# An encoder block on one core: the transpose of a feed-forward unit's result moved one weight chunk later

## The chip, the cores and the metric

The kernel runs on one core of a Trainium2 chip. The metric is the device time of one execution in microseconds (us). TensorE (PE) multiplies, VectorE (DVE) and ScalarE (ACT) do elementwise work, GpSimd (POOL) a few small things, and SyncE (SP) issues most loads. Each engine works through its own instructions in the order in which the program issues them.

## What is computed

One layer of an encoder over 256 positions of width 2048, in float32: a gated feed-forward with half weight, a mixer, a second gated feed-forward with half weight, and a final norm.

```python
def swiglu(h, w_gate, w_up, w_down):
    return (jax.nn.silu(h @ w_gate) * (h @ w_up)) @ w_down

x = x + 0.5 * swiglu(rmsnorm(x, ffn1_norm), ffn1_w_gate, ffn1_w_up, ffn1_w_down)
...   # mixer: input projection, pooling branch, convolution branch, gates, output projection
x = x + 0.5 * swiglu(rmsnorm(x, ffn2_norm), ffn2_w_gate, ffn2_w_up, ffn2_w_down)
out = rmsnorm(x, final_norm)
```

The feed-forward is 5632 wide; its three weights are 2048x5632, 2048x5632 and 5632x2048. The change touches the two feed-forward stages alone.

## The kernel before

**Numbers in two words.** Every operand of a product is split into a high word (a rounded copy, made by a cast on ScalarE) and a low word (the rest, made by a subtraction on VectorE): `hi_lo`, lines 154 and 156. A product is three matmuls: high by high (data high, weight high), then data high by weight low, then data low by weight high. In the profile weights are `raw` as loaded, then `wh` and `wl`.

**Units and chunks.** The weights stream through in chunks of two tiles of 128x1024. A `Unit` is a run of chunks that adds up to 256x1024 results in PSUM: a gate unit has 8 chunks (512 gate columns and the 512 up columns beside them), a half of a down projection 8 chunks (6 in the last one). A feed-forward stage consists of gate units 0 to 10; behind gate units 4 and 8, and at the end, two halves of a down projection take the hidden units made so far. In all gate units but unit 0, and in the down projections but the last, chunks 0 and 2 are calculated as a 2x2 block product with seven multiplications (`SEVEN = (0, 2)`): `split_seven` makes four sums of weight blocks on VectorE (line 194, tile `sum`) and splits three tiles (the first weight tile, the sums as `exth`/`extl`, the second weight tile). Such a chunk has 21 matmuls (line 278), any other 24 (line 257). In unit 1 of each stage the seven products come in another order: those that need the sums first.

**The order of work.** It is written out by hand. `run` goes through the chunks; for chunk i it issues, in this order, the loads of chunk i+2 on SP's queue, the splitting of chunk i+1, the functions that were left for i with `at(i, ...)`, and the matmuls of chunk i. So each engine has the splitting of the next chunk ahead of the side work of the present one. There are 5 buffers for loaded tiles and 4 each for `wh` and `wl`, two chunks' worth.

**A hidden unit's way.** When a gate unit u is done, at its chunk 7, `gate_done_seven` adds the partial results on VectorE (line 431), applies Silu on ScalarE (line 432) and multiplies (line 436): two tiles `h` of 128x512, one for each half of the positions. The down projection needs them transposed. `turn` (line 386) has ScalarE separate the 16-bit halves of `h` (line 391, tile `halves`) and issue a DMA transpose (line 393, tile `turned`), once for each of the two tiles. `put` (line 397) has ScalarE join the transposed halves (line 403, tile `hy`) and splits the result in two words into `ht` (`hi_lo`). For some units (those with u mod 4 equal to 0 or 1) `put` leaves `e_forms` (line 303) for the chunk after: four subtractions on VectorE (line 308, tile `e`) and their splitting into `hEh` and `hEl`, for the seven-product chunks of the down projection.

In time: `turn` of unit u stands in chunk 0 of the unit that follows. `gate_early` runs in chunk 3 of a gate unit, takes what was turned last, and leaves its `put` for chunk 4; `e_forms` comes in chunk 5. Unit 10 has no gate unit behind it; its `put` is left by `rest_of_hidden`, in chunk 3 of the last down projection.

Of the kernel before, what the change touches and what calls it, by code (L numbers as in the profile page):

```python
# [18 lines left out]
FF = 5632  # L19
# [7 lines left out]
C = 512  # L27
# [55 lines left out]
def encoder_kernel(ctx: ExitStack, tc: tile.TileContext, x, xT, vecs, rows, pool_m,  # L83
# [30 lines left out]
    def at(i, fn):  # L114

        side.setdefault(i, []).append(fn)
# [36 lines left out]
    def hi_lo(src, h, l=None):  # L153
        nc.scalar.copy(out=h, in_=src)  # L154
        if l is not None:
            nc.vector.tensor_tensor(out=l, in0=src, in1=h.bitcast(F32), op=ALU.subtract)  # L156
        return h, l
# [145 lines left out]
    def e_forms(dst, even, odd):  # L303

        e = stg.tile([P, 4, P], F32, tag="sg", name=f"e{Pos.now}")
        a11, a21, a12, a22 = even[:, :P], even[:, P:], odd[:, :P], odd[:, P:]
        for n, (a, b) in enumerate(((a11, a21), (a21, a22), (a11, e[:, 1, :]), (a12, e[:, 2, :]))):
            nc.vector.tensor_tensor(out=e[:, n, :], in0=a, in1=b, op=ALU.subtract)
        hi_lo(e, *dst)
# [67 lines left out]
    def ffn_units(w_g, w_d, xt, xE, rs, residual_done, tail=None):  # L377
# [8 lines left out]
        def turn(u, hs):  # L386

            turned = []
            for t in range(NT):
                halves = ffn["pool"].tile([P, 2, C], U16, tag=f"halves{t}", name=f"halves{Pos.now}_{t}")  # L390
                nc.scalar.copy(out=halves, in_=hs[t].bitcast(U16).rearrange("p (f w) -> p w f", w=2))  # L391
                z = ffn["pool"].tile([P, 8, P], U16, tag=f"turned{t}", name=f"turned{Pos.now}_{t}")
                nc.scalar.dma_start_transpose(out=z, in_=halves.rearrange("p w f -> p (w f)"))  # L393
                turned.append(z)
            waiting.append((u, turned))

        def put(u, turned):

            y = ffn["pool"].tile([P, 4, T], F32, tag="y", name=f"hy{Pos.now}")
            whole = y.bitcast(U16).rearrange("p j (t w) -> p w j t", w=2)  # L400
            for t in range(NT):
                for w in range(2):
                    nc.scalar.copy(out=whole[:, w, :, t * P:(t + 1) * P], in_=turned[t][:, 4 * w:4 * w + 4, :])  # L403
            hi_lo(y, *ffn["ht"][u % GROUP])
            for c in SEVEN:
                if c // 2 == u % GROUP:
                    q = c % 2 * 2
                    at(Pos.now + 1, lambda c=c, q=q: e_forms(ffn["hE"][c], y[:, q, :], y[:, q + 1, :]))

        def hidden_tile(t):  # L410
            return stg.tile([P, C], F32, tag="h", name=f"h{Pos.now}_{t}")

        def gate_done(u):
            def done(acc):
                hs = []
                for t in range(NT):
                    sg = stg.tile([P, C], F32, tag="sg", name=f"sg{Pos.now}_{t}")
                    h = hidden_tile(t)
                    nc.scalar.activation(sg, acc[t][:, 0, :], AF.Silu, scale=rs[:, t:t + 1])
                    nc.vector.scalar_tensor_tensor(out=h, in0=acc[t][:, 1, :], scalar=rs[:, t:t + 1],  # L420
                                                   in1=sg, op0=ALU.mult, op1=ALU.mult)
                    hs.append(h)
                at(Pos.now + 1, lambda: turn(u, hs))
            return done

        def gate_done_seven(u):
            def done(acc):
                hs = []
                for t in range(NT):
                    z = ffn[f"t{t}"]  # L430
                    nc.vector.tensor_tensor(out=z, in0=acc[t], in1=z, op=ALU.add)  # L431
                    nc.scalar.activation(z[:, 0, :], z[:, 0, :], AF.Silu, scale=rs[:, t:t + 1])
                for t in range(NT):
                    z = ffn[f"t{t}"]
                    h = hidden_tile(t)
                    nc.vector.scalar_tensor_tensor(out=h, in0=z[:, 1, :], scalar=rs[:, t:t + 1],
                                                   in1=z[:, 0, :], op0=ALU.mult, op1=ALU.mult)
                    hs.append(h)
                at(Pos.now + 1, lambda: turn(u, hs))
            return done  # L440

        def shared_parts():

            z0, z1 = ffn["t0"], ffn["t1"]
            nc.scalar.copy(out=z0[:, 0, :], in_=ps[:, B_P1, :])
            for out, a, b, op in ((z1[:, 1, :], ps[:, B_P6, :], z0[:, 0, :], ALU.subtract),
                                  (z0[:, 1, :], ps[:, B_P5, :], z1[:, 1, :], ALU.add),
                                  (z1[:, 0, :], ps[:, B_P7, :], z1[:, 1, :], ALU.subtract),
                                  (z1[:, 1, :], z0[:, 1, :], ps[:, B_P7, :], ALU.subtract)):
                nc.vector.tensor_tensor(out=out, in0=a, in1=b, op=op)  # L450

        def gate_early():
            shared_parts()
            if waiting:
                u, turned = waiting.pop()
                at(Pos.now + 1, lambda: put(u, turned))

        def into_residual(t, half, part):
            xs = X[t][:, half * W2:(half + 1) * W2]
# [37 lines left out]
        for u in range(units):  # L497
            if u:
                add_unit(Unit(w_g[u], KD, lhs_of(xt), gate_done_seven(u), forms=forms_of(lhs_of(xt), xE),
                              early=gate_early, seven=SEVEN, start=(lambda: None) if u == 1 else None))  # L500
            else:
                first = Unit(w_g[u], KD, lhs_of(xt), gate_done(u))
                add_unit(first)
                at(len(stream), open_hidden)
            if u and u % GROUP == 0:
                add_down(u // GROUP - 1, 4 * GROUP, False)
# [519 lines left out]
```

## Time and profile before

| | |
|---|---|
| median of 3 runs | 1961.78 us (1959.55 to 1965.18) |
| profiled execution | 1962.23 us, span 1960.4 us |
| granted TensorE clock, mean | 0.997 |
| DMA transposes | 44, from issue to landing 7.5 / 10.0 / 12.4 us (min, median, max) |
| loads of feed-forward weights | 512 KB each, 4.4 us (gate and up) and 4.3 us (down) median to landing |

The span runs from the first to the last recorded instruction. In rows of instructions stand start, duration, engine, line, operation, what it writes and reads, the shapes, how many were merged, and in brackets how long the engine stood idle before it and what ended that. Rows of the chain of waits have start, duration and what; the chain is followed back from the last instruction. `ACTq` and `SPq` are the sequencers of ScalarE and SyncE, which issue DMAs. A matmul's row is longer than the step from one to the next, since they overlap.

### The profile page before, as it was taken

What the parts mean: (1) busy time and instruction counts of PE and PEld (TensorE: products, weight loads), DVE (VectorE), ACT (ScalarE), POOL (GpSimd) and SP (SyncE); (2) the same over time, 40 slices, a digit from 0 to 9 for tenths busy, and PEclk for the clock granted to TensorE, in tenths of its full rate; (3) what the DMA queues carried; (4) which work ended last, traced back from release to release, by engine and by line L of the source; (5) the groups of instructions that cost most, each with busy time, mean ns of one, the idle gap of its engine ahead of it and who ended that gap; (6) DMA issues with size and microseconds to landing.
All of it is one profiled execution on the core that took longest, in us unless ns stands there. A gap on an engine that the chain in (4) does not pass through costs nothing.

```text
span 1960.4 us, 23002 instructions
## 1 busy us (share of the span) xinstructions
PE 1924.6 (98%) x8504; PEld 1579.2 (81%) x8504; DVE 1517.1 (77%) x1740; ACT 1065.3 (54%) x1215; POOL 11.3 (1%) x22
## 2 busy tenths in 40 slices
PE   9999999999999999999999999999999999999998
PEld 7777788778787888888888888877778877778776
DVE  6788787888888655888898766688788788888865
ACT  6655645555555555454444545556654556654554
POOL 0000000000000000000000000000000000000000
PEclk9999999999999999999999999999999999999999
DMA  8777766777767756556666555567786577676774
GB/s 312 196 193 199 193 227 198 200 210 201 197 201 196 221 183 203 193 197 213 200 209 198 191 183 185 185 197 196 194 210 226 195 204 203 193 209 205 196 200 156
DMA packets 152608, 395.42 MB, mean 202 GB/s; under 512 B 58384, under 2 KB 58640, under 8 KB 152240
## 3 DMA queue, kind: packets, MB, share of 16 engines
q1 hardware_dynamic: 104688, 378.45, 58.6%
q10 hardware_dynamic: 46752, 11.68, 8.1%
q0 software_dynamic: 1056, 3.83, 0.6%
q8 instruction: 66, 1.08, 0.2%
q14 instruction: 46, 0.38, 0.1%
HBM read 380.28 MB, written 2.10 MB: 195 GB/s over the span
## 4 chain that ended last, share of the span: by engine, by line
PE 83%; ACT 6%; DVE 4%; DMA 3%; issue 2%; ACTq 2%; DVEq 0%; POOLq 0%; POOL 0%
PE ps L257 73%; PE ps L278 9%; ACT wh L154 2%; DMA raw<-in_w_g 2%; ACTq L393 2%; DVE extl L156 2%; ACT exth L154 2%; ACT halves L391 1%; DMA raw<-in_w_d 1%; DVE wl L156 1%; PE ps L344 1%; ACT hy L403 0%; PE ps L758 0%; DVE part L431 0%; DMA xrh<-in_xT 0%
## 5 line engine op out<-in xcount | busy, mean ns | idle before, releaser
L156 DVE TENSOR_TENSOR wl<-raw,wh 128x1024 fp32r<-128x1024 f32 (+1 forms) x706 | 842.4, 1219 | 294.1 <-ACT wh L154 293.1
L154 ACT CAST wh<-raw 128x1024 fp32r<-128x1024 f32 (+1 forms) x706 | 726.2, 1048 | 615.5 <-PE ps L257 314.2
L257 PE MATMUL ps<-wh,xt1h 128*128 128x512 f32 x544 | 168.5, 391 | 1.2 <-ACT wh L154 1.2
L257 PE MATMUL ps<-wl,xt1h 128*128 128x512 f32 x544 | 168.4, 390 | 0.2
L257 PE MATMUL ps<-wh,xt1l 128*128 128x512 f32 x544 | 168.4, 391 | 0.0
L257 PE MATMUL ps<-wh,xt3h 128*128 128x512 f32 x544 | 167.7, 389 | 0.0
L257 PE MATMUL ps<-wh,xt3l 128*128 128x512 f32 x544 | 167.5, 389 | 0.0
L257 PE MATMUL ps<-wl,xt3h 128*128 128x512 f32 x544 | 167.5, 389 | 0.0
L257 PE MATMUL ps<-wh,xt2h 128*128 128x512 f32 x448 | 138.4, 390 | 0.0
L257 PE MATMUL ps<-wh,xt2l 128*128 128x512 f32 x448 | 138.0, 389 | 0.0
L257 PE MATMUL ps<-wl,xt2h 128*128 128x512 f32 x448 | 138.0, 389 | 0.0
L257 PEld LDWEIGHTS ps<-wh,xt1h 128*128 128x128 f32 x544 | 102.6, 189 | 23.1 <-ACT wh L154 1.7
L257 PEld LDWEIGHTS ps<-wl,xt1h 128*128 128x128 f32 x544 | 102.3, 188 | 22.2 <-DVE wl L156 1.0
L257 PEld LDWEIGHTS ps<-wh,xt1l 128*128 128x128 f32 x544 | 102.3, 188 | 21.8 <-DVE xt1l L336 0.5
L257 PEld LDWEIGHTS ps<-wl,xt3h 128*128 128x128 f32 x544 | 102.1, 188 | 21.2
L257 PEld LDWEIGHTS ps<-wh,xt3l 128*128 128x128 f32 x544 | 102.1, 188 | 21.2
L257 PEld LDWEIGHTS ps<-wh,xt3h 128*128 128x128 f32 x544 | 102.0, 188 | 21.1
L156 DVE TENSOR_TENSOR extl<-sum,exth 128x1536 fp32r<-128x1536 f32 x56 | 98.5, 1759 | 18.3 <-ACT exth L154 15.7
L257 PEld LDWEIGHTS ps<-wh,xt2l 128*128 128x128 f32 x448 | 84.1, 188 | 17.6
L257 PEld LDWEIGHTS ps<-wl,xt2h 128*128 128x128 f32 x448 | 84.1, 188 | 17.6
L617 DVE SCALAR_TENSOR_TENSOR conv<-gluT,vec,conv 128x241 f32<-128x241 f32 (+14 forms) x240 | 97.0, 472 | 0.0
L257 PEld LDWEIGHTS ps<-wh,xt2h 128*128 128x128 f32 x448 | 83.3, 188 | 16.6
(239 smaller groups left out, 2902.2 us busy)
## 6 DMA issues: line engine op xcount, KB each, us to landing
raw<-in_w_g SPq DMA_DIRECT2D x350, 512.0 KB, 4.4
raw<-in_w_d SPq DMA_DIRECT2D x176, 512.0 KB, 4.3
raw<-in_w_in SPq DMA_DIRECT2D x112, 512.0 KB, 4.0
raw<-in_w_out SPq DMA_DIRECT2D x32, 512.0 KB, 4.2
raw<-in_w_pp SPq DMA_DIRECT2D x16, 512.0 KB, 3.6
raw<-in_w_cp SPq DMA_DIRECT2D x16, 512.0 KB, 3.6
row<-in_rows POOLq DMA_DIRECT2D x7, 512.0 KB, 4.0
X<-in_x SPq DMA_DIRECT2D x2, 1024.0 KB, 8.5
```

Of the source, the lines that this page charges most:

```text
L154: nc.scalar.copy(out=h, in_=src)
L156: nc.vector.tensor_tensor(out=l, in0=src, in1=h.bitcast(F32), op=ALU.subtract)
L257: nc.tensor.matmul(u.acc[t + c if u.tail and t else t][:, c, :], lhsT=a, rhs=b[:, c * C:(c + 1) * C], start=(t, c) not in u.begun, stop=k ...
L278: nc.tensor.matmul(ps[:, b, :], lhsT=x_, rhs=w_, start=where not in u.begun, stop=b < B_11 and cc == u.seven[-1] and n == 2)
L344: nc.tensor.transpose(out=b[:, j * T + t * P: j * T + (t + 1) * P], in_=src_of(j, t), identity=ident)
L391: nc.scalar.copy(out=halves, in_=hs[t].bitcast(U16).rearrange("p (f w) -> p w f", w=2))
L393: nc.scalar.dma_start_transpose(out=z, in_=halves.rearrange("p w f -> p (w f)"))
L617: nc.vector.scalar_tensor_tensor(out=dst, in0=src, scalar=w, in1=dst, op0=ALU.mult, op1=ALU.add)
```

## The change

`turn` is left for chunk 1 of the unit that follows instead of chunk 0, except for the last gate unit (`FF // C - 1` is 10), where it stays in chunk 0. `put` from `gate_early` is left for chunk 5 instead of chunk 4, and with it `e_forms` comes in chunk 6 instead of 5. `put` of unit 10 stays.

```diff
@@ gate_done, gate_done_seven
-                at(Pos.now + 1, lambda: turn(u, hs))
+                at(Pos.now + (1 if u == FF // C - 1 else 2), lambda: turn(u, hs))
@@ gate_early
             if waiting:
                 u, turned = waiting.pop()
-                at(Pos.now + 1, lambda: put(u, turned))
+                at(Pos.now + 2, lambda: put(u, turned))
```

More of the change, by code (lines that the diff above doesn't have):

```diff
@@ L438, in done @@
                     hs.append(h)
-                at(Pos.now + 1, lambda: turn(u, hs))
+                at(Pos.now + (1 if u == FF // C - 1 else 2), lambda: turn(u, hs))
             return done
```

## The prediction

> **What bounds the kernel now.** I read the page first (busy shares, shares of the chain of waits), then the chain in order of time, then each engine's instructions around one unit. Chunks of a unit are counted 0 to 7 here.
>
> ```profile
> PE 1924.6 (98%) x8504; PEld 1579.2 (81%) x8504; DVE 1517.1 (77%) x1740; ACT 1065.3 (54%) x1215; POOL 11.3 (1%) x22
> PE 83%; ACT 6%; DVE 4%; DMA 3%; issue 2%; ACTq 2%; DVEq 0%; POOLq 0%; POOL 0%
> ```
>
> TensorE bounds it, but 17% of the chain runs elsewhere although PE counts as 98% busy. The chain shows where (start, duration, what):
>
> ```profile
> 275.99 4.76 PE ps L278 x21
> 318.15 4.76 PE ps L278 x21
> ...
> 403.95 1.37 PE ps L278 x6
> 415.14 1.77 DVE extl L156
> 416.95 3.46 PE ps L278 x14
> 447.61 1.37 PE ps L278 x6
> ```
>
> The unit at 275.99 (second half of a down projection; nothing is turned in it) takes 318.15 - 275.99 = 42.16 us and never leaves PE. The unit at 403.95 (gate unit 7, in which unit 6 is turned) takes 43.66: 1.50 more, lost in chunk 2, a seven-product chunk that waits for the low words of its sums (extl). Within that unit:
>
> ```profile
> 403.79 0.39 PE L278 MATMUL ps<-wh,xt1h 128*128 128x512 f32 x1
> 402.82 2.39 DVE L431 TENSOR_TENSOR part<-ps,part 128x1024 f32<-128x1024 f32 x2
> 405.87 1.99 ACT L154 CAST wh<-raw 128x1024 fp32r<-128x1024 f32 x2
> 406.94 2.36 DVE L156 TENSOR_TENSOR wl<-raw,wh 128x1024 fp32r<-128x1024 f32 x2 [0.18 <-ACT wh L154]
> 407.76 1.04 ACT L391 COPY halves<-h 128x1024 uint16<-128x1024 uint16 x1
> 408.83 1.25 ACTq L393 DMA_TRANSPOSE turned<-halves  x1
> 410.12 1.05 ACT L391 COPY halves<-h 128x1024 uint16<-128x1024 uint16 x1 [1.32 <-DVE sum L194]
> 411.20 1.37 ACTq L393 DMA_TRANSPOSE turned<-halves  x1
> 411.38 0.69 DVE L194 TENSOR_TENSOR sum<-sum,raw 128x512 f32<-128x512 f32 x1
> 412.68 1.05 ACT L154 CAST wh<-raw 128x1024 fp32r<-128x1024 f32 x1 [1.51 <-DVE sum L194]
> 415.14 1.76 DVE L156 TENSOR_TENSOR extl<-sum,exth 128x1536 fp32r<-128x1536 f32 x1
> 420.25 0.61 PE L257 MATMUL ps<-wh,xt1h 128*128 128x512 f32 x2
> 420.70 0.39 PE L257 MATMUL ps<-wl,xt1h 128*128 128x512 f32 x1
> ```
>
> ScalarE splits chunk 1 (405.87), then runs the turn: two copies and two DMA triggers that hold it, 407.76 to 412.68 = 4.92 us. Only then come the casts of chunk 2, though VectorE's sums for them end at 412.07. Extl is done at 416.90, and chunk 3 starts at 420.25 instead of 418.75.
>
> **The change part by part.** It adds and removes no instruction. Of 22 turns 20 move (units 0 to 9 of both feed-forward stages; the last unit's stays), and so do 20 put's with their e_forms.
>
> (a) The turn leaves the place ahead of chunk 2's casts. They follow the sums, as they do where no turn is near:
>
> ```profile
> 441.16 0.69 DVE L194 TENSOR_TENSOR sum<-sum,raw 128x512 f32<-128x512 f32 x1
> 441.89 1.48 ACT L154 CAST exth<-sum 128x1536 fp32r<-128x1536 f32 x1 [0.27 <-DVE sum L194]
> 443.28 1.05 ACT L154 CAST wh<-raw 128x1024 fp32r<-128x1024 f32 x1
> ```
>
> The sums end at 441.85; exth starts 0.04 later, the last cast starts 1.43 and ends 2.48 after the sums. In unit 7 the casts are over at 412.07 + 2.48 = 414.55; extl, 0.04 behind an exth that ends at 413.59, ends near 415.4. PE wants extl with the eighth matmul of chunk 2; chunk 2 starts at 403.79 + 4.76 + 5.44 = 413.99 (chunks 0 and 1 by their own lengths), the eighth 7/21 of 4.76 later, 415.58. So the stall of 1.50 goes.
>
> (b) What is late next: the turn now stands ahead of chunk 3's casts on ScalarE, and these are queued behind both triggers. It starts 0.10 before the last cast's end (as at 407.76 against 405.87 + 1.99), takes 4.92, and chunk 3's first cast starts 2.48 - 0.10 + 4.92 = 7.30 after the sums, 419.37. The cast (1.05), 0.04 to VectorE, the subtraction (1.22) and 0.04 to PE put the first low words (wl) at sums + 9.65 = 421.72. Before, PE read them at 420.70. So every unit whose VectorE runs on time loses 1.02: the wait of 1.50 in chunk 2 is replaced by some 2.5 in chunk 3. The idle time of ScalarE that the turn used to fill (from 407.86 until the sums are done) now stays empty.
>
> The triggers' cost at the new place has bounds from the rows:
>
> ```profile
> L393 ACTq DMA_TRANSPOSE turned<-halves x44: 1247/1284/2375, 56.8 to 1890.3; - x44
> L148 SPq DMA_DIRECT2D raw<-in_w_g x354: 327/328/817, 0.7 to 1864.4; - x177
> ```
>
> From 0.33 each (SP's plain trigger) to 2.38; I take the 1.25 and 1.37 of unit 7, since the same instruction took no less than 1.247 in 44 cases.
>
> (c) The two units with the seven-product order turned round (unit 1 of each stage) lose more before and gain:
>
> ```profile
> 59.33 0.69 DVE L194 TENSOR_TENSOR sum<-sum,raw 128x512 f32<-128x512 f32 x1
> 71.71 0.62 PE L257 MATMUL ps<-wh,xt1h 128*128 128x512 f32 x2
> 1282.70 0.69 DVE L194 TENSOR_TENSOR sum<-sum,raw 128x512 f32<-128x512 f32 x1
> 1293.42 0.62 PE L257 MATMUL ps<-wh,xt3h 128*128 128x512 f32 x2
> ```
>
> Chunk 3's wl come at 60.02 + 9.65 = 69.67 and 1293.04, against a read at 71.71 + 0.45 and 1293.42 + 0.45: -2.5 and -0.8, together -3.3.
>
> (d) The put moves from chunk 4 to chunk 5 and ends closer to the next unit. Its place on ScalarE is right behind a cast that waits for PE to free a buffer (338.58), so it moves by exactly one chunk, 5.44. Rows of a put with e_forms (339.55) and of one without (its subtraction at 430.61):
>
> ```profile
> 338.58 1.06 ACT L154 CAST wh<-raw 128x1024 fp32r<-128x1024 f32 x1 [1.67 <-PE ps L257]
> 339.55 2.64 ACT L403 COPY hy<-turned 128x512 uint16<-128x512 uint16 x4
> 343.30 1.23 DVE L156 TENSOR_TENSOR ht0l<-hy,ht0h 128x1024 fp32r<-128x1024 f32 x1 [2.40 <-ACT ht0h L154]
> 348.54 0.69 DVE L156 TENSOR_TENSOR hEl<-e,hEh 128x512 fp32r<-128x512 f32 x1 [0.69 <-ACT hEh L154]
> 351.77 0.69 DVE L194 TENSOR_TENSOR sum<-raw,raw 128x512 f32<-128x512 f32 x1
> 359.00 2.57 DVE L431 TENSOR_TENSOR part<-ps,part 128x1024 f32<-128x1024 f32 x2
> ...
> 430.61 1.23 DVE L156 TENSOR_TENSOR ht0l<-hy,ht0h 128x1024 fp32r<-128x1024 f32 x1 [2.01 <-ACT ht0h L154]
> 438.99 0.68 DVE L194 TENSOR_TENSOR sum<-raw,raw 128x512 f32<-128x512 f32 x1
> 447.64 1.22 DVE L431 TENSOR_TENSOR part<-ps,part 128x1024 f32<-128x1024 f32 x1 [0.21 <-PE ps L257]
> ```
>
> Without e_forms: the put's subtraction ends at 430.61 + 1.23 + 5.44 = 437.28; chunk 7's two subtractions follow (2.36 for a pair as at 406.94, each start some 0.1 ahead of the end before it) and the sums for the next unit's chunk 0 start at 439.45 instead of 438.99, 0.46 late. VectorE waits only 0.21 for PE at L431 afterwards, so L431, and all that hangs on it (Silu, h, the next unit's sums), is 0.25 late.
>
> With e_forms: hEl ends at 349.23 + 5.44 = 354.67, and in the new order chunk 7's subtractions are already done, so the sums that are queued behind hEl on VectorE start at 354.67 instead of 351.77: 2.9 late. The reserve is 2.57 - 2.39 = 0.2 (the wait inside the pair at 359.00, against 402.82), so L431 is 2.7 late. From L431 to chunk 3's wl the chain on ScalarE and VectorE has no slack (a, b), so the slip adds in full to the 1.02.
>
> Who is hit: e_forms belong to puts of units 0, 1, 4, 5, 8, 9, done in gate units 1, 2, 5, 6, 9, 10. The next unit is gate 2, 3, 6, 7, 10 (five a stage); behind gate 10 comes the last down projection, whose first chunk has no sums: no cost. Puts without e_forms are followed by gate 4, 8 and two first halves of a down projection: four a stage.
>
> (e) At no cost: the transposes' traffic. The loads that share the DMA engines with it are now those of chunk 5 instead of chunk 4. The triggers move by 414.45 - 407.76 = 6.7, PE by 5.44 plus 1.0 or more, so the reserve stays as it is; if it were gone, each us of lateness would be a us of PE. The put's own reads shift with the triggers in the same way. On SP's and POOL's queues nothing is reordered.
>
> **Sum.** Eight units at 1.02 + 0.25 = 1.27: +10.2. Ten at 1.02 + 2.7 = 3.72: +37.2. Part (c): -3.3. Together +44.1. The profiled run took 1962.2 us (1.8 outside its span of 1960.4), 0.4 over the median 1961.8, to which I add: **2006 us**, 2.2% slower.
>
> **Rivals.**
> - The knock-on of (d) is absorbed. For it: VectorE is idle for 23% of the span. Against: L431 has just 0.2 to spare. Then 18 x 1.02 - 3.3 = +15: 1977.
> - The trigger is mostly a wait for SP, and at the new place it takes SP's 0.33: the turn shrinks by 0.92 + 1.04 = 1.96. Eight units gain 0.69, ten lose 1.76: -5.5 + 17.6 and -4.3 for (c), +8: 1970. Against: 1.247 shortest and 1.284 median leave little that varies. The Trainium skill, Perfetto Trace Analysis (Per-engine timelines), says that a trigger's recorded span holds a wait for a descriptor generator shared between sequencers besides the generation itself; the trace's narrow spread speaks for the generation.
> - Not slower: the turn fits behind chunk 2's casts. The point that decides: chunk 3's wl on time at 418.75 + 0.45, which needs a turn of 4.92 - 2.52 = 2.4 us or less, about its two copies (1.04 + 1.05) alone. Then the 1.5 vanishes in eight units (about -1.25 each), the ten pay 2.7 - 1.5, (c) gains 5: -10 + 12 - 5 = -3: 1959; with the knock-on small too, down to 1962 - 36 = 1926. Against: ScalarE sat idle through both triggers (1.32 beside 410.12).
> - Worse: triggers nearer 2.38 or late loads add 1 us and more to each of 20 units: 2025 and up.
>
> **How the numbers follow.** Chances: forecast 0.62 (own range 1995 to 2018: a good third of the 27 us of slip less, or 0.6 us a unit more for restarts of PE and slower triggers), knock-on absorbed 0.15, short trigger 0.05, fits 0.10, worse 0.08. The range leaves out the last two: 1968 to 2018. 0.3% is about what a measurement here can tell from no change. Faster: 0.07 of the case that fits; same: its 0.03 and 0.02 more; slower: the rest, 0.88.
>
> **What would show it.** Right: in the chain, pieces of 27.20 us (chunks 3 to 7 in one) break into chunk 3 and later, with ScalarE's cast and VectorE's wl ahead of chunk 3; L393 starts some 11.7 us or more after a unit's start instead of 5.0; extl no longer in the chain after gate 7 or 8; L194 right behind hEl; gate 7 at 47.4 us, gate 8 at 44.9. Wrong, if L393 were short at its new place, if L431 still waited for PE after a put with e_forms, or if another engine's wait stood ahead of chunk 3.

## The result and the profile after

The changed kernel takes 2013.17 us (median of 4 runs, 2010.34 to 2020.40) against 1962.42 before: ratio 1.0264, 95% interval 1.0233 to 1.0296. The profiled execution took 2011.69 us, its span 2009.9. The page's busy shares and the shares of its chain of waits:

```profile
PE 1943.0 (97%) x8504; PEld 1582.4 (79%) x8504; DVE 1513.1 (75%) x1740; ACT 1067.6 (53%) x1215; POOL 11.3 (1%) x22
PE 64%; DVE 15%; ACT 12%; issue 5%; ACTq 3%; DMA 1%; DVEq 0%; POOLq 0%; POOL 0%
```

The busy times are those of before within a per cent: no work was added. What changed is who ends last. TensorE's share of the chain fell from 83% to 64%, VectorE's rose from 4% to 15% and ScalarE's from 6% to 12%.

The same stretch as in the prediction, gate unit 7 (start, duration, engine, line, what, idle time before it; a choice of rows):

```profile
411.13 0.69 DVE L156 TENSOR_TENSOR hEl<-e,hEh 128x512 fp32r<-128x512 f32 x1 [0.69 <-ACT hEh L154]
411.74 0.68 DVE L194 TENSOR_TENSOR sum<-raw,raw 128x512 f32<-128x512 f32 x1
417.30 0.39 PE L278 MATMUL ps<-wh,xt1h 128*128 128x512 f32 x1
418.97 2.35 DVE L431 TENSOR_TENSOR part<-ps,part 128x1024 f32<-128x1024 f32 x2
421.37 0.50 PE L278 MATMUL ps<-exth,xt1h 128*128 128x512 f32 x1 [1.20 <-DVE part L431]
421.98 1.98 ACT L154 CAST wh<-raw 128x1024 fp32r<-128x1024 f32 x2
427.50 0.69 DVE L194 TENSOR_TENSOR sum<-sum,raw 128x512 f32<-128x512 f32 x1
428.30 1.49 ACT L154 CAST exth<-sum 128x1536 fp32r<-128x1536 f32 x1 [0.34 <-DVE sum L194]
430.64 1.04 ACT L391 COPY halves<-h 128x1024 uint16<-128x1024 uint16 x1
431.71 1.25 ACTq L393 DMA_TRANSPOSE turned<-halves  x1
434.08 1.25 ACTq L393 DMA_TRANSPOSE turned<-halves  x1
435.42 3.90 ACT L154 CAST wh<-raw 128x1024 fp32r<-128x1024 f32 x4 [1.38 <-PE ps L278]
436.50 4.63 DVE L156 TENSOR_TENSOR wl<-raw,wh 128x1024 fp32r<-128x1024 f32 x4 [3.78 <-ACT wh L154]
436.52 0.73 PE L257 MATMUL ps<-wh,xt1h 128*128 128x512 f32 x2 [1.42 <-ACT wh L154]
437.78 0.73 PE L257 MATMUL ps<-wl,xt1h 128*128 128x512 f32 x2 [0.53 <-DVE wl L156]
464.68 0.39 PE L278 MATMUL ps<-wh,xt1h 128*128 128x512 f32 x1
```

The unit takes 464.68 - 417.30 = 47.38 us. The sums for its chunk 0 (411.74) start right behind hEl. L431, in which the unit before is finished, ends at 421.32, that is 4.0 after the unit's start instead of 1.4. TensorE waits for it already in chunk 0 (421.37, 1.20 us). The turn now follows the casts of chunk 2, and chunk 3's casts (435.42) follow the turn; TensorE waits for their high words (1.42 us) and then for their low words (0.53 us). The chain runs through these steps and comes back to TensorE only in chunk 3 (pieces between the rows are left out):

```profile
419.05 2.28 DVE part L431 x2
421.98 1.04 ACT wh L154
424.19 1.22 DVE wl L156
427.50 0.70 DVE sum L194
429.69 1.05 ACT wh L154
430.74 0.95 ACT halves L391
431.71 1.25 ACTq L393
434.08 1.25 ACTq L393
435.42 1.05 ACT wh L154
436.50 1.24 DVE wl L156
437.78 10.76 PE ps L257 x46
```

Two things are new against before. The transposes land much sooner (10.0 us median before):

```profile
DMA to landing us min/median/max: 3.1/3.5/10.5
```

And TensorE's granted clock is at half speed in more places. The windows below (length, busy time of each engine, then PEclk, DMA share and GB/s) lie in gate unit 6, the last two in gate unit 7:

```profile
385.90:389.30 3.40, 1.50 (x6) 0.77 (x5) 1.80 (x2) 2.88 (x4) 0.00 (x0) 1.00 0.71 201
389.30:392.70 3.40, 3.40 (x9) 2.64 (x9) 3.40 (x4) 1.50 (x3) 0.00 (x0) 0.50 0.75 227
433.70:437.10 3.40, 1.98 (x9) 1.12 (x7) 0.60 (x1) 2.02 (x3) 0.00 (x0) 1.00 1.06 232
437.10:440.50 3.40, 2.87 (x13) 2.24 (x13) 3.40 (x4) 2.79 (x5) 0.00 (x0) 1.00 0.67 193
```

In unit 6 a window in which TensorE was busy for 1.50 of 3.40 us is followed by one at clock 0.50, in which 9 matmuls are done instead of 15 or 16. In unit 7 the same wait falls across the border of two windows, 1.98 of 3.40 is busy, and the clock stays at 1.00. Unit 6 takes 417.30 - 368.30 = 49.00 us, 1.62 more than unit 7. From the first gate unit with sums (52 us) to shortly before the end the trace of the changed kernel has six such half-clock stretches, at 164.0, 256.2, 389.3, 1502.1, 1635.2 and 1904.8, that of the kernel before one, at 66.1.

### The profile page after: what moved, and what is told of

The parts are those of the page before. It is cut to its first block, busy times and chain, and to the rows that moved or that the text cites. A ratio compares the mean times of both kernels' runs of the same rounds, so it can differ in the third digit from the quotient of the medians.

```text
span 2009.9 us, 23004 instructions
## 1 busy us (share of the span) xinstructions
PE 1943.0 (97%) x8504; PEld 1582.4 (79%) x8504; DVE 1513.1 (75%) x1740; ACT 1067.6 (53%) x1215; POOL 11.3 (1%) x22
## 4 chain that ended last, share of the span: by engine, by line
PE 64%; DVE 15%; ACT 12%; issue 5%; ACTq 3%; DMA 1%; DVEq 0%; POOLq 0%; POOL 0%
PE ps L257 59%; DVE wl L156 6%; ACT wh L154 4%; PE ps L278 4%; DVE sum L194 4%; ACTq L393 3%; ACT hy L403 3%; ACT halves L391 2%; DVE part L431 2%; DVE extl L156 2%; ACT exth L154 2%; DVE raw L194 1%; DMA raw<-in_w_d 1%; PE ps L344 1%; ACT ht0h L154 1%
```

## The experiments

Theory A is the prediction's: a wait of 1.0 us more for each turn, because it now blocks chunk 3 instead of chunk 2, and a slip of VectorE caused by the late put, mostly by e_forms. To this the profile after added a third part: half-clock stretches caused by longer waits of TensorE.

**The turn alone.** The put stays in chunk 4.

```diff
-                at(Pos.now + 2, lambda: put(u, turned))
+                at(Pos.now + 1, lambda: put(u, turned))
```

> The turn one chunk later, the put left in chunk 4. Theory A (two separate costs: the turn now stands ahead of chunk 3's casts, +1.0 us in 18 units and -3.3 us in the two others; the late put with e_forms costs the next unit 2.7 us): only the first is left, 1962 + 15 = 1977 us, up to 1985 with a few half-clock stretches of TensorE; VectorE's line 431 again ends some 1.4 us after a unit's start. Theory B (the late turn alone makes the next unit late, the place of the put does not matter): 2005 us or more.

Measured: 1985.6 us against 1964.2, ratio 1.0107 (1.0086 to 1.0129), +21. VectorE around the start of gate unit 7 (405.78), which stands behind a put with e_forms:

```profile
405.78 0.39 PE L278 MATMUL ps<-wh,xt1h 128*128 128x512 f32 x1
404.63 2.57 DVE L431 TENSOR_TENSOR part<-ps,part 128x1024 f32<-128x1024 f32 x2
```

L431 is done 1.4 us after the unit's start, and its 2.57 us hold a short wait for TensorE again (2.35 without one). The slip is gone although the turn is late: the late turn alone does not bring it, and theory B, which the expectation sets against A, falls. 15 of the 21 us are the forecast term; the clock, 0.994 against 0.997 in the profiles, is some 6 us more of 1982 (five half-clock stretches, counted as above, instead of one).

**The put alone.** The turn stays in chunk 0.

```diff
-                at(Pos.now + (1 if u == FF // C - 1 else 2), lambda: turn(u, hs))
+                at(Pos.now + 1, lambda: turn(u, hs))
```

> The turn left in chunk 0, the put one chunk later (e_forms in chunk 6). Theory A: the wait of 1.5 us in chunk 2 stays, and the slip of VectorE comes on top, 10 x 2.7 + 8 x 0.25 = +29: 1991 us, up to 1999 with half-clock stretches. The effects of this kernel and of the one with the turn alone add up to that of the whole change. Theory B: 1962 us.

Measured: 1989.8 us, ratio 1.0132 (1.0114 to 1.0150), +26. Around the start of gate unit 7 (410.26):

```profile
404.09 0.69 DVE L156 TENSOR_TENSOR hEl<-e,hEh 128x512 fp32r<-128x512 f32 x1 [0.69 <-ACT hEh L154]
404.70 0.68 DVE L194 TENSOR_TENSOR sum<-raw,raw 128x512 f32<-128x512 f32 x1
411.93 2.35 DVE L431 TENSOR_TENSOR part<-ps,part 128x1024 f32<-128x1024 f32 x2
```

The slip is here without the late turn: L431 ends 4.0 us after the unit's start. The two halves of the change nearly add up, 21 + 26 = 47 of the 51 us.

**e_forms taken out of the way.** The whole change, with e_forms in chunk 4 of the next unit; those of units 8 and 9, which no product reads, are left out.

```diff
-                if c // 2 == u % GROUP:
+                if c // 2 == u % GROUP and u < 2 * GROUP:
                     q = c % 2 * 2
-                    at(Pos.now + 1, lambda c=c, q=q: e_forms(...))
+                    at(Pos.now + 7, lambda c=c, q=q: e_forms(...))
```

> The whole change, but e_forms leave chunk 6 for chunk 4 of the unit that follows (those of units 8 and 9, which no product reads, are left out); the put itself stays in chunk 5. Theory A (the subtractions of e_forms that stand ahead of the next unit's sums on VectorE are what costs 2.45 of the 2.7 us): the ten hit units fall to the loss of the eight others, 18 x 1.27 - 3.3 = +20: 1982 us, up to 1990. Rival: the put's own copies, 5.4 us later, are what makes VectorE late: 2006 to 2013 us.

Measured: 1990.0 us against 1964.2, ratio 1.0131 (1.0113 to 1.0150): +26 where the whole change has +51, so 25 us less, with 24.5 expected for ten units at 2.45. Gate unit 7 starts at 407.27, and

```profile
406.58 2.35 DVE L431 TENSOR_TENSOR part<-ps,part 128x1024 f32<-128x1024 f32 x2
```

ends 1.66 after that, 0.24 later than before the change: the small slip that the put's own subtraction was to cost. The +26 is 6 us over the +20 of theory A, about what the clock costs: it is at 0.993, as in the whole change, with five half-clock stretches instead of one.

**The wait filled with products of zeros.** Whole change, with six matmuls of zeros added to an accumulator ahead of chunk 3.

```diff
+        if u.seven and cc == 3 and Pos.turned == i - 2:
+            zero = ffn["zero"]
+            for _ in range(6):
+                nc.tensor.matmul(u.acc[0][:, 0, :], lhsT=zero[:, :P], rhs=zero, start=False, stop=False)
```

> The whole change, with six products of zeros (added to an accumulator, about 1.36 us of TensorE) ahead of chunk 3 in the 20 units with a moved turn, to fill the wait for the first high words there. Theory A (the half-clock stretches of 3.4 us, five more than before in the profile, come from TensorE's idle time around chunk 3; each costs 1.6 us): at most two stretches are left inside the span, 2013 - 8 + 2.4 (two units have no such wait and pay for the products) = 2007 us. Rival (they come from the DMA traffic or by chance): five or six stretches again, 2013 to 2016 us.

Measured: 2006.7 us, ratio 1.0215 (1.0194 to 1.0237), with 120 matmuls more. The intervals of this ratio and of the whole change's just touch; the mean granted clock of the profiled executions says it more sharply. The whole change:

```profile
core 0: 2009.9 us, clock 0.993
```

The kernel with the products of zeros:

```profile
core 0: 2009.4 us, clock 0.998
```

All four runs of this kernel have 0.998 or 0.999. The four of the whole change have 0.994, 0.993, 0.992 and 0.990, and in that order they take 2010.3, 2011.7, 2014.7 and 2020.4 us: 0.004 of 2010 is 8 us of the 10 between the first and the last. The three kernels above agree: the two with the turn in chunk 1 have 0.992 to 0.995, the one with the turn in chunk 0 has 0.997 and 0.998. So idle TensorE time around chunk 3 causes the half-clock stretches, and the stretches cause most of the spread. The profiled run, 2011.2, is this kernel's slowest; with a span only 0.5 us shorter than that of the whole change, it does not show the gain in time, which rests on the other three (2006.3 to 2006.7).

**The turn cut in two.** From the kernel before: first tile in chunk 0, second in chunk 1, put in chunk 4.

```diff
-                at(Pos.now + 1, lambda: turn(u, hs))
+                at(Pos.now + 1, lambda: turn(u, hs, (0,)))
+                at(Pos.now + (1 if u == FF // C - 1 else 2), lambda: turn(u, hs, (1,)))
```

> The kernel before, with the turn cut in two: the first tile's copy and trigger stay in chunk 0, the second tile's go to chunk 1; put in chunk 4 as before. Theory A (what costs is one block of 4.9 us on ScalarE in front of a splitting; half a block, 2.4 us, fits both into the gap before chunk 2's casts and behind them before chunk 3's): waits in chunks 2 and 3 of 0.3 us a unit at most, 1962 - 33 = 1930 us, no half-clock stretches behind the start; up to 1945 if the put then has to wait for the later transpose. Rival (a turn in chunk 1 is harmful as such, or a second split of the work costs a wait of its own): each of 18 units keeps 1.5 us or more, 1960 us or more.

Measured: 1944.8 us, ratio 0.9909 (0.9889 to 0.9930), faster, but 15 us short of the 1930. Thirteen of the 18 units that lost 1.5 us or more now lose under 0.5. The other five lose 12 us together, most of it to late loads, which the expectation had not allowed for; here in gate unit 3, where chunk 5's casts and the put behind them wait:

```profile
164.24 1.05 ACT L154 CAST wh<-raw 128x1024 fp32r<-128x1024 f32 x1 [4.57 <-DMA raw<-in_w_g]
166.44 2.68 ACT L409 COPY hy<-turned 128x512 uint16<-128x512 uint16 x4
```

(In one of the five, at 1309.48, a trigger of 2.95 us in chunk 1 holds ScalarE instead.) The transposes land hardly sooner than before:

```profile
DMA to landing us min/median/max: 4.3/9.5/11.9
```

**Late, but in short blocks.** Tiles in chunks 1 and 2, put in chunk 5, e_forms in chunk 4 of the next unit (those of units 8 and 9 left out).

```diff
+            for t in range(NT):
+                at(Pos.now + (1 if u == FF // C - 1 else 2 + t), lambda t=t: turn(u, hs, (t,)))
```

> The late order of the whole change with short blocks: first tile's copy and trigger in chunk 1, second tile's in chunk 2, put in chunk 5, e_forms in chunk 4 of the next unit (those of units 8 and 9 left out, as nothing reads them). Theory A (lateness in itself costs nothing but the 0.25 us a unit of the put): 1962 - 33 + 5 = 1934 us, up to 1945. Rival (the later place is what costs): 1975 to 1990 us, as with the whole turn in chunk 1.

Measured: 1964.6 us, ratio 1.0013 (1.0003 to 1.0024). A miss: neither the 1934 of theory A nor the rival's 1975 and more. The waits for the turn are gone, but a new one stands in their place. ScalarE and VectorE ahead of the start of gate unit 8 (446.08):

```profile
430.59 0.62 ACT L154 CAST hEh<-e 128x512 fp32r<-128x512 f32 x1 [4.89 <-DVE e L308]
431.12 2.00 ACT L154 CAST wh<-raw 128x1024 fp32r<-128x1024 f32 x2
433.02 2.65 ACT L409 COPY hy<-turned 128x512 uint16<-128x512 uint16 x4
447.42 2.35 DVE L437 TENSOR_TENSOR part<-ps,part 128x1024 f32<-128x1024 f32 x2
```

The cast hEh now stands ahead of chunk 6's casts and the put, and waits 4.89 us for VectorE's e. The put is late again, and L437 (the old L431) ends 3.7 us after the unit's start. In the third experiment, with e_forms in the same chunk 4, the cast hEh waited 2.98 us at this place; in all it waits 39.1 us here against 23.2 there. Late loads take a part too: in gate unit 4 of the first stage, where there are no e_forms to wait for, ScalarE waits 5.27 us for a load ahead of the put (214.51). How the loss divides between the two is not shown. The run says nothing against theory A's mechanism, but it does not show that lateness is free.

**Copies first, triggers later.** From the kernel before: both copies stay in chunk 0, both triggers go to chunk 1, put in chunk 4.

```diff
         def turn(u, hs):
...
+                at(Pos.now + 1, lambda: issue(u, apart))
+        def issue(u, apart):
+            for t in range(NT):
...
+                nc.scalar.dma_start_transpose(out=z, in_=apart[t].rearrange("p w f -> p (w f)"))
```

> The kernel before, with both copies of the turn left in chunk 0 (2.1 us, in ScalarE's idle time ahead of chunk 2's casts) and both triggers moved to chunk 1; put in chunk 4. Theory A: the copies end before the casts can start, the triggers take 2.6 us behind them, so chunks 2 and 3 wait 0.3 us a unit at most; and triggered together and later, the transposes land in 3 to 5 us as in the changed kernel, not in 9.5 as with the triggers a chunk apart, so loads are not late either: 1962 - 33 = 1930 us. Rival (triggers issued ahead of the loads' gap, or late loads again): 1940 to 1950 us, as with the turn cut in two.

Measured: 1931.1 us (1926.0 to 1933.0) against 1960.2, ratio 0.9842 (0.9824 to 0.9860): 1.6% faster than before and 4% faster than the changed kernel. The page's shares of the chain:

```profile
PE 95%; ACT 1%; DVE 1%; DMA 1%; issue 1%; ACTq 0%; DVEq 0%; POOLq 0%; POOL 0%
```

ScalarE in gate unit 7:

```profile
394.84 1.99 ACT L391 COPY halves<-h 128x1024 uint16<-128x1024 uint16 x2
397.87 1.06 ACT L154 CAST wh<-raw 128x1024 fp32r<-128x1024 f32 x1 [1.04 <-DVE raw L194]
399.27 1.48 ACT L154 CAST exth<-sum 128x1536 fp32r<-128x1536 f32 x1 [0.34 <-DVE sum L194]
399.40 1.32 ACTq L402 DMA_TRANSPOSE turned<-halves  x1
400.66 1.04 ACT L154 CAST wh<-raw 128x1024 fp32r<-128x1024 f32 x1
400.76 1.53 ACTq L402 DMA_TRANSPOSE turned<-halves  x1
402.39 2.95 ACT L154 CAST wh<-raw 128x1024 fp32r<-128x1024 f32 x3 [0.69 <-ACT wh L154]
```

The landing of the transposes, by tile:

```profile
DMA to landing us min/median/max: 3.3/4.9/11.8
```

Both copies fit into ScalarE's idle time. The triggers, with no copy between them to wait for, run on its sequencer while the engine casts: two triggers of 2.85 us leave it idle for only 0.69. The expectation had counted them as 2.6 us of ScalarE. The loads are on time as well: over the whole kernel ScalarE's weight casts wait 4.0 us for loads of gate and up weights, against 44.4 before and 43.8 with the turn cut in two.

## Why the prediction was right

- **The turn blocks chunk 3 (b).** In gate unit 7 the sums end at 428.19 and TensorE reads the first wl at 437.78, 9.59 later; 9.65 was forecast. Alone this part costs the 15 us and the clock on top. Extl is no longer what TensorE waits longest for (0.45 us in this unit, against 1.42 for chunk 3's high words), as (a) said.
- **The put's slip (d).** L431 is late by 4.0 - 1.4 = 2.6 us behind a put with e_forms (2.7 forecast) and by 0.24 behind one without (read in the third experiment; 0.25 forecast). Gate unit 7 came out at 47.38 us, forecast 47.4, and gate unit 8 (464.68 to 509.62) at 44.9, as forecast; the put alone cost 26 us, forecast 29. The prediction put the whole loss ahead of chunk 3; where it shows is different. Behind a put with e_forms TensorE waits in chunk 0 already, for the late L431 (chunk 1 of gate unit 7 starts at 423.58, 6.28 after the unit's start instead of 4.76), and again in chunks 2 and 3. All of these waits come from the same late chain, so the size of the loss is as forecast.
- **The rivals.** Absorbed knock-on (1977), a trigger that shrinks to SP's 0.33 (1970; the shortest stayed 1.25) and a turn that fits (1959) are all excluded: L393 lasted what it had lasted, and L431 found nothing to hide behind. Late loads (2025 and up) did not come; they became fewer.
- **The term that was missing: the clock.** The forecast for the median was 2006, 7 us short. The mean clock of 0.993 over 2009.9 us is 14.1 us of lost clock, that of 0.997 over 1960.4 is 5.9: 8.2 us more. The clocks are rounded to 0.001, which leaves this uncertain by up to 2 us; five stretches more at the 1.62 of unit 6 make 8.1. The prediction had "restarts of PE and slower triggers" as reasons for up to 12 us more, but not the clock. The row of PEclk in the page, all nines in both kernels, is too coarse to show stretches of 3.4 us; the windows show them. Without the clock the span grew by 49.5 - 8.2 = 41 us, 3 less than the sum of 44. So the 2006 came as near as it did partly by luck: two terms that the sum does not have, the clock and the loads of the next point, work against each other.
- **The transposes' traffic (e).** "The reserve stays as it is" was wrong in size, on the harmless side: the landing fell from 10.0 to 3.5 us. It is the trigger's place that does it: 3.5 again with the turn alone moved, 9.8 with the put alone. The weight loads gain too: ScalarE's casts wait 4.0 us in all for gate and up loads, 44.4 before. Gate unit 3 of the first stage, which took 44.75 us before because of a late load, takes 48.99 with a half-clock stretch in it, 2.6 more without the 1.62 where 3.72 was forecast; so about 1 of the 3 us is seen here.

The Trainium skill, TensorE: Matmul & The Clock Gate (Part 1 and its part on oscillation), describes a gate that halves the clock after an idle window of about 3.4 us that runs freely, and gives gaps of more than 3.4 us as what to avoid. The windows here agree on the half clock and on the free-running 3.4 us, but no fully idle window was needed: ahead of the six stretches TensorE was still busy for 1.46 to 1.75 us of the 3.4. Windows of the same kernel with 1.81 or 1.98 were followed by the full clock. That is no sharp rule of busy time: with the put alone a window at 1930.30 with only 1.45 us busy was so too, and no run here shows why.

## What to carry to other kernels

Before moving a block of work on an in-order engine, write down what stands behind it in the new place and how much reserve that has; moving 4.9 us in front of another splitting with less than 2.5 us of reserve only moves the wait, while the engine's old gap stays empty. Order within the block can matter more than its place: copies into the gap, and DMA triggers behind casts that the engine still has to run, gained 29 us where the plain move lost 51. Work that hangs on the moved step (here e_forms, two steps later) has to be followed to the next stage too.

## What the runs showed of the hardware that was not expected

- A wait of TensorE of about 2 us in a window of 3.4 us cost a further 1.6 us at half clock (gate unit 6), or nothing where the window's border cut it (gate unit 7); with part of the wait filled by zero products the mean clock was 0.998 instead of 0.993.
- DMA transposes of 256 KB land in 3.5 us (median; 4.9 in the last experiment) when both are triggered in chunk 1, behind the casts, and in 8.7 to 10.0 us when triggered in chunk 0 or a chunk apart, with weight loads (512 KB, 4.2 us median in the changed kernel) under way. Loads are delayed then too: ScalarE's casts wait 35 to 44 us in all for gate and up loads, against 4.0.
- A trigger hardly holds ScalarE if the engine has casts issued ahead of it to run (0.69 us idle for two triggers of 2.85 in the last experiment); it does when it waits for a copy and the next copy stands behind it (1.32 us idle for a trigger of 1.25 before).
